# Three short matmuls between block 0 and the first paired block of an out-projection

## The chip, the cores and the metric

The kernel runs on one core of one Trainium2 chip. The metric is the device time of one execution in microseconds (us). Before the change three runs gave 822.88, 823.33 and 823.69 us, median 823.33. The profile is of one further execution of the same program.

## What is computed

The reference is one decoder block for a sequence of 512 tokens and a model width of 2048, in float32. Cut to what matters here:

```python
h = _rmsnorm(x, norm_g[l])
proj = h @ w_in[l]                       # queries, keys, values, gates, z
...                                      # two groups of attention heads -> y_a, y_b
x = x + jnp.concatenate([y_a, y_b], axis=-1) @ w_out[l]
...
return _rmsnorm(x, final_g)
```

The change lies in the product with `w_out`, a 512 x 2048 times 2048 x 2048 product, the last large stage.

## The kernel before, in words

All products of float32 data are made from pairs of words in fp32r, a high and a low one. `mm3` (line 121) issues three matmuls for one product: line 122 takes high by high, line 123 high by low, line 124 low by high. In the out-projection the stationary operand of a matmul is a 128 x 128 piece of the activations (`yh`, `yl`, `ph`, `pl`, `uh`, `ul`, `qh`, `ql`), and the moving operand is a piece of the weights (`whi`, `wlo`). Each matmul comes with its own load of the stationary operand; the trace shows it as LDWEIGHTS on a row of its own, PEld, and it runs beside the matmul before.

The weights come in by DMA as units of 128 x 1024 float32. ScalarE copies a unit to its high word, VectorE subtracts to get the low word (`load_unit`, line 85; `split_to`, line 957, for the out-projection; lines 958 and 959). The words go into tiles that are 1088 words wide per partition, and `words(place)` (line 82) chooses where in the tile the 1024 used words begin: `MOVING, EVEN, STILL = 0, 16, 32` (line 29). So the place sets at which word address a unit begins; `p_words` (line 964) does the same with tiles 2112 wide.

The 2048 output columns are four blocks of 512 (variable `n`).

- **Block 0** (the loop over `u` in range(8) behind `acc = banks(0)`) is a plain product: for each of 16 pieces of the contraction and each of four row tiles one `mm3`, its matmuls 512 columns wide. In between, `combos` (line 971) builds sums and differences of the activations: `p`, `u`, `q`.
- **Blocks 1, 2 and 3** (the loop `for n in range(1, 4)`) use a scheme with seven instead of eight half-size products on 2 x 2 sub-blocks ("12", "21", "22", "p", "u", "q", "w"). Each is one call of `product` (line 1123), or two calls for a half each in block 3: 8 pieces times 2 row tiles times 3 matmuls = 48 matmuls, each 256 columns wide. That makes 7 x 48 = 336 matmuls in a block and 1008 in the three. These are the paired blocks.

The first product of block 1 is "p", into the PSUM tile `ba` (named `oa` in the profile). Its stationary operands are `ph` and `pl`, the first unit of weights is `u3`, converted by `halves` (line 1072) while block 0 still runs.

Behind each product VectorE adds PSUM into sums in SBUF, and the next weights are converted. At the end of block 3 the rows are scaled by their norm (lines 1004 to 1036) and written out by DMA (line 1020).

Order: within an engine the instructions stand in an order that the framework's scheduler chose; `tc.issue_after(x)` puts what follows behind instruction `x` on its engine. In block 3 the order is nearly written out by hand in this way (`do`, `mm`). `recent["mm"]` is the last matmul that `mm3` issued.

Of the kernel before, what the change touches and what calls it, by code (L numbers as in the profile page):

```python
# [17 lines left out]
P = 128  # L18
# [17 lines left out]
def hybrid_block(ctx, tc, xT, xtm, w0, w1s, w2s, wz, wq, wkb, wo0, wos, cw1, cw2, cpos, rope, tabs, sinks, gT, fg, out):  # L36
    nc = tc.nc
    pe, act, dve, pool = nc.tensor, nc.scalar, nc.vector, nc.gpsimd
# [39 lines left out]
    def raw():  # L78
        raws[0] += 1
        return weights(f"raw{raws[0] % 3}")  # L80
# [38 lines left out]
    recent = {}  # L119
# [56 lines left out]
    for k in range(KT):  # L176
# [7 lines left out]
        for i in range(4):  # L184
            o = i * P
# [140 lines left out]
    for u in range(KT // 2):  # L326
# [15 lines left out]
        for j in range(2):  # L342
            k = 2 * u + j
            for i in range(4):
                o = j * 512 + i * P
# [562 lines left out]
    for i in range(8):  # L908
# [8 lines left out]
        if i == 7:  # L917
# [3 lines left out]
            yh = [so1.tile([P, S], F32R, name=f"yh{f}") for f in range(16)]  # L921
# [121 lines left out]
    def banks(n):  # L1043
        if n % 2 == 0:
            return [psf1.tile([P, S], F32, name="oa", tag="oa") for t in range(2)] + \
                   [psp.tile([P, S], F32, name="pj", tag="pj") for t in range(2)]
        return [psf2.tile([P, S], F32, name="oa", tag="oa") for t in range(4)]
# [24 lines left out]
    def halves(raw, to=None):  # L1072
        hi, lo = to or words(MOVING)
        split_to(hi, lo, raw)
        return hi, lo

    def as_pair(b):
        return b.rearrange("p (t c) -> p t c", c=256)

    fgt = []  # L1080
    for n in range(1, 4):
        xs.append([late(2 * n - 2 + T) for T in range(2)])
        src = wos[n - 1]
        ba, bb, bx, bc = [as_pair(b) for b in banks(n)]
# [3 lines left out]
        def scratch():  # L1088
            return so.tile([P, 2, 256], F32, name="e", tag="e", bufs=3)

        def load(dst, quarter, g):
            last["dma"] = nc.sync.dma_start(dst, src[quarter, g]).ins
            return dst
# [29 lines left out]
        def product(bank, units, op, new, ts=(0, 1)):  # L1123
            for m in range(8):
                hi, lo = units[m // 4]
                cs = slice((m % 4) * 256, (m % 4) * 256 + 256)
                ah, al = ops[op, m]
                for t in ts:
                    r = slice(t * P, (t + 1) * P)
                    mm3(bank[:, t, :], ah[:, r], al[:, r], hi[:, cs], lo[:, cs], new and m == 0 and t == ts[0],  # L1130
                        m == 7 and t == ts[-1], not new)
# [3 lines left out]

        u3 = [halves(load(raw(), 0, g)) for g in range(2)]
        e3 = scratch()
        if n < 3:
            product(ba, u3, "p", True)
            act.activation(e3, ba, AF.Copy)  # L1140
# [232 lines left out]
```

## Time and profile before

| | |
|---|---|
| three runs, us | 822.88, 823.33, 823.69 |
| the profiled execution, us | 822.97 |
| its span, first to last instruction, us | 821.2 |
| mean granted TensorE clock | 0.997 |
| TensorE (PE) busy, us | 808.1 |
| VectorE (DVE) busy, us | 665.9 |
| ScalarE (ACT) busy, us | 484.4 |
| block 0 of the out-projection, us from the span's start | 652.5 to 694.7 |
| paired blocks, us from the span's start | 694.7 to 813.4 |
| last sums, norms and writes, us | 813.4 to 821.2 |

How to read it: the span lies inside the device time, which has 822.97 - 821.2 = 1.8 us more around it. A row of the timeline has the start, the length, the engine, the line in the kernel, the operation and the tiles, out<-in. Matmuls are pipelined: the length of a row is that of one matmul from its start to the end of its drain, and the next one starts long before that. What a stream of matmuls costs is therefore the distance from one start to the next, called the pitch here. An engine that is busy 98% by this count can still run at two different pitches.

Where two addresses are compared, they are in words of 4 bytes within a partition, and only the remainder by 64 is given. The distance of a matmul is the start address of its moving operand less the start address of the stationary operand that is loaded while it runs, that is, of the next matmul's. The addresses of the tiles are those of the built program; the profile doesn't show them.

### The profile page before, as it was taken

What the parts mean: (1) busy time and instruction counts of PE and PEld (TensorE: products, weight loads), DVE (VectorE), ACT (ScalarE), POOL (GpSimd) and SP (SyncE); (2) the same over time, 40 slices, a digit from 0 to 9 for tenths busy, and PEclk for the clock granted to TensorE, in tenths of its full rate; (3) what the DMA queues carried; (4) which work ended last, traced back from release to release, by engine and by line L of the source; (5) the groups of instructions that cost most, each with busy time, mean ns of one, the idle gap of its engine ahead of it and who ended that gap; (6) DMA issues with size and microseconds to landing.
All of it is one profiled execution on the core that took longest, in us unless ns stands there. A gap on an engine that the chain in (4) does not pass through costs nothing.

```text
span 821.2 us, 14128 instructions
## 1 busy us (share of the span) xinstructions
PE 808.1 (98%) x5278; PEld 736.2 (90%) x5278; DVE 665.9 (81%) x1326; ACT 484.4 (59%) x1026; POOL 66.6 (8%) x54
## 2 busy tenths in 40 slices
PE   9999999999999999999999999999999999999996
PEld 8788898989999999999988888888888888999996
DVE  7869786867889899899877598887777899768895
ACT  6734456564767787777665465544553747453545
POOL 4500002010000000000011211011001000000000
PEclk9999999999999999999999999999999999999998
DMA  9655886898321332432732322222223167596835
GB/s 330 203 197 167 288 301 192 285 346 296 99 91 29 114 105 89 144 109 77 262 114 83 116 78 77 69 87 54 75 81 100 52 180 278 128 264 154 275 57 205
DMA packets 52116, 128.30 MB, mean 156 GB/s; under 512 B 4944, under 2 KB 17232, under 8 KB 52048
## 3 DMA queue, kind: packets, MB, share of 16 engines
q1 hardware_dynamic: 50032, 120.59, 43.9%
q0 software_dynamic: 1728, 6.29, 4.5%
q8 instruction: 41, 0.67, 0.3%
q10 hardware_dynamic: 288, 0.52, 0.2%
q14 instruction: 27, 0.22, 0.1%
HBM read 110.31 MB, written 17.07 MB: 155 GB/s over the span
## 4 chain that ended last, share of the span: by engine, by line
PE 92%; ACT 2%; DVE 2%; DMA 1%; issue 1%; POOL 1%; SPq 0%; DVEq 0%
PE pj L124 17%; PE pj L123 17%; PE pj L122 16%; PE oa L122 5%; PE oa L123 5%; PE oa L124 5%; PE bank L124 4%; PE bank L122 4%; PE bank L123 4%; PE sp L557 3%; PE tp L595 2%; PE tp L879 2%; DMA xr<-xT 1%; PE spb L844 1%; PE spb L845 1%; PE bank L236 1%
## 5 line engine op out<-in xcount | busy, mean ns | idle before, releaser
L124 PE MATMUL pj<-xh,wlo 128*128 128x512 f32 (+1 forms) x560 | 194.9, 348 | 1.8 <-DVE wlo L635 1.8
L122 PE MATMUL pj<-xh,whi 128*128 128x512 f32 (+1 forms) x560 | 194.6, 348 | 0.0
L123 PE MATMUL pj<-xl,whi 128*128 128x512 f32 (+1 forms) x560 | 194.5, 347 | 0.0
L96 DVE TENSOR_TENSOR wlo<-raw,whi 128x1024 fp32r<-128x1024 f32 (+2 forms) x102 | 115.6, 1137 | 34.2 <-ACT whi L95 33.5
L95 ACT ACTIVATE whi<-raw 128x1024 fp32r<-128x1024 f32 (+1 forms) x101 | 95.0, 944 | 77.1 <-PE pj L123 23.4
L124 PEld LDWEIGHTS pj<-xh,wlo 128*128 128x128 f32 x560 | 105.4, 188 | 15.0 <-DVE wlo L635 2.4
L123 PEld LDWEIGHTS pj<-xl,whi 128*128 128x128 f32 x560 | 105.3, 188 | 13.2 <-issue 0.9
L122 PEld LDWEIGHTS pj<-xh,whi 128*128 128x128 f32 x560 | 105.3, 188 | 12.2
L635 DVE TENSOR_TENSOR wlo<-raw,whi 128x1024 fp32r<-128x1024 f32 x49 | 59.5, 1220 | 9.5 <-ACT whi L634 9.4
L634 ACT ACTIVATE whi<-raw 128x1024 fp32r<-128x1024 f32 x49 | 51.2, 1055 | 21.7 <-PE pj L123 10.7
L122 PE MATMUL oa<-whi,yh 128*128 128x256 f32 (+1 forms) x168 | 50.5, 302 | 0.6 <-ACT yh L954 0.6
L123 PE MATMUL oa<-wlo,yh 128*128 128x256 f32 (+1 forms) x168 | 50.8, 302 | 0.0
L124 PE MATMUL oa<-whi,yl 128*128 128x256 f32 (+1 forms) x168 | 50.2, 302 | 0.0
L858 ACT ACTIVATE ttb<-ttb,sums 128x256 f32<-128x256 f32 (+1 forms) x64 | 30.1, 471 | 27.0 <-DVE sums L851 26.5
L525 ACT ACTIVATE ph<-tp 128x512 fp32r<-128x512 f32 x56 | 32.3, 592 | 14.5 <-PE tp L595 8.4
L123 PE MATMUL bank<-wlo,xh 128*128 128x256 f32 (+1 forms) x128 | 40.1, 315 | 0.0
L124 PE MATMUL bank<-whi,xl 128*128 128x256 f32 (+1 forms) x128 | 39.8, 313 | 0.0
L526 DVE TENSOR_TENSOR pl<-tp,ph 128x512 fp32r<-128x512 f32 x56 | 37.9, 685 | 1.8 <-ACT ph L525 1.6
L122 PE MATMUL bank<-whi,xh 128*128 128x256 f32 (+1 forms) x128 | 36.5, 317 | 1.3 <-ACT whi L95 1.3
L122 PE MATMUL bank<-xh,whi 128*128 128x512 f32 x96 | 36.7, 392 | 0.4 <-ACT whi L95 0.3
L123 PE MATMUL bank<-xl,whi 128*128 128x512 f32 x96 | 36.9, 390 | 0.0
L573 ACT ACTIVATE tt<-tt,sums 128x128 f32<-128x128 f32 (+3 forms) x64 | 35.3, 554 | 1.5 <-DVE sums L563 1.4
(357 smaller groups left out, 2173.9 us busy)
## 6 DMA issues: line engine op xcount, KB each, us to landing
raw<-wz SPq DMA_DIRECT2D x36, 512.0 KB, 3.8
raw<-wq SPq DMA_DIRECT2D x28, 512.0 KB, 3.7
raw<-cw SPq DMA_DIRECT2D x16, 512.0 KB, 4.8
raw<-wos SPq DMA_DIRECT2D x12, 512.0 KB, 4.4
rw<-wos SPq DMA_DIRECT2D x10, 512.0 KB, 5.4
xr<-xT SPq DMA_DIRECT2D x16, 256.0 KB, 4.8
raw<-w SPq DMA_DIRECT2D x8, 512.0 KB, 4.1
fd<-ft SPq DMA_DIRECT2D x4, 1024.0 KB, 6.1
```

Source lines behind the costliest of these rows:

```text
L95: last["hi"] = act.activation(hi[:, :width], rw[:, :width], AF.Copy).ins
L96: last["lo"] = dve.tensor_tensor(out=lo[:, :width], in0=rw[:, :width], in1=hi[:, :width].bitcast(F32), op=ALU.subtract).ins
L122: pe.matmul(ps, ah, bh, start=first, stop=False, skip_group_check=go_on)
L123: pe.matmul(ps, ah, bl, start=False, stop=False, skip_group_check=go_on)
L124: recent["mm"] = pe.matmul(ps, al, bh, start=False, stop=last, skip_group_check=go_on).ins
L525: act.activation(ph, tp, AF.Copy)
L526: dve.tensor_tensor(out=pl, in0=tp, in1=ph.bitcast(F32), op=ALU.subtract)
L557: pe.matmul(sp[:, a:b], qq[:, qs], kk[0][:, ko:ko + b - a], start=pi == 0, stop=pi == 2)
L573: act.activation(tv, tv, AF.Exp, bias=mn[:, i, 1 + w:2 + w], scale=-1.0, accum_out=dn[:, i, 1 + w:2 + w])
L634: act.activation(hi, src, AF.Copy)
L635: last["lo"] = dve.tensor_tensor(out=lo, in0=src, in1=hi.bitcast(F32), op=ALU.subtract).ins
L858: act.activation(tv, tv, AF.Exp, bias=mn[:, e, v:v + 1], scale=-1.0, accum_out=dn[:, e, v:v + 1])
```

## The change

A helper `step_in` issues three matmuls behind the last one of block 0 and ahead of the "p" product of block 1. All three have the same stationary operand, the first 128 columns of `yh[1]`, and as moving operand 256 columns of the same tile that begin 48, 64 and 32 words further on. They write the first half of the PSUM tile `ba`, each with start and stop set; the first matmul of the "p" product starts that tile anew, so nothing of theirs is kept. The engines' other instructions and their order are the same in both programs.

```diff
@@ -1077,6 +1077,11 @@
     def as_pair(b):
         return b.rearrange("p (t c) -> p t c", c=256)
 
+    def step_in(bank):
+        with tc.issue_after(recent["mm"]):
+            for o in (48, 64, 32):
+                pe.matmul(bank[:, 0, :], yh[1][:, 0:P], yh[1][:, o:o + 256], start=True, stop=True)
+
     fgt = []
     for n in range(1, 4):
         xs.append([late(2 * n - 2 + T) for T in range(2)])
@@ -1135,6 +1140,8 @@
 
         u3 = [halves(load(raw(), 0, g)) for g in range(2)]
         e3 = scratch()
+        if n == 1:
+            step_in(ba)
         if n < 3:
             product(ba, u3, "p", True)
             act.activation(e3, ba, AF.Copy)
```

In the changed program the three stand on line 1083, between the last line 124 of block 0 and the first line 122 of block 1. The lines behind them move down by five, and those behind the call by seven.

## The prediction

> **What bounds the kernel now.** I read the page first, then the busy time by stage, then the timeline of TensorE.
>
> ```profile
> PE 808.1 (98%) x5278; PEld 736.2 (90%) x5278; DVE 665.9 (81%) x1326; ACT 484.4 (59%) x1026; POOL 66.6 (8%) x54
> PE 92%; ACT 2%; DVE 2%; DMA 1%; issue 1%; POOL 1%; SPq 0%; DVEq 0%
> ```
>
> The first row is busy time by engine, the second the chain that ended last: TensorE holds 92% of it. The paired blocks and what follows them (columns: stretch, its length, then busy time of PE, PEld, DVE, ACT and POOL with counts, granted clock, DMA share and rate):
>
> ```profile
> 694.73:813.40 118.67, 118.67 (x1009) 118.66 (x1007) 94.46 (x117) 60.13 (x88) 8.73 (x10) 1.00 0.66 186
> ```
>
> ```profile
> 813.40:821.20 7.80, 0.22 (x2) 0.01 (x1) 1.80 (x5) 2.14 (x5) 0.00 (x0) 0.71 0.40 149
> ```
>
> In the paired blocks (first row) PE is busy in every microsecond at full clock (1.00), and behind it comes a tail of 7.8 us that starts when PE ends. So the time can only fall there if the matmuls follow each other faster. Whether they can is told by the pitch, the distance between starts. The first two rows are the first and the last of the 1008 paired matmuls; the other two are the first and the last of 116 matmuls of an earlier stage, of the same shape and at the same distance (48):
>
> ```profile
> 694.73 0.28 PE L122 MATMUL oa<-whi,ph 128*128 128x256 f32 x1
> ...
> 813.34 0.28 PE L124 MATMUL oa<-whi,ql 128*128 128x256 f32 x1
> ```
>
> ```profile
> 104.61 0.28 PE L122 MATMUL bank<-whi,xh 128*128 128x256 f32 x1
> ...
> 117.64 0.28 PE L236 MATMUL bank<-whi,F 128*128 128x256 f32 x1
> ```
>
> The paired blocks run at (813.34 - 694.73) / 1007 = 117.8 ns. The earlier stage runs at (117.64 - 104.61) / 115 = 113.3 ns. Neither stream has a pause. So the same kind of matmul has **two steady paces**, 4.5 ns apart, at one clock and one distance of addresses; by their rows neither width, type nor distance decides which. What decides must be history, and there the trace can be read like an experiment, since the head loop often mixes in a matmul at another distance.
>
> **What the three matmuls do.** Their distances follow from the diff alone: the stationary operand begins at the tile's start, the moving one 48, 64 and 32 words behind, so 48, 0 and 32 by the remainder. After them "p" begins at 48 again, as all 1008 do. The question is what the series 48, 0, 32, 48 does to a stream at the slow pace. The head loop has it, where one attention matmul (L601) stands between projection matmuls: by the addresses of the tiles in the built program the load for L601 makes the distance of the matmul ahead of it 0, and the load behind L601 makes its own 32; all others there have 48.
>
> ```profile
> 352.53 0.28 PE L123 MATMUL pj<-xl,whi 128*128 128x256 f32 x1
> ...
> 354.65 0.28 PE L123 MATMUL pj<-xl,whi 128*128 128x256 f32 x1
> 354.77 0.28 PE L601 MATMUL op<-ph,VH 128*128 128x256 f32 x1
> 354.89 0.28 PE L124 MATMUL pj<-xh,wlo 128*128 128x256 f32 x1
> ...
> 355.59 0.28 PE L124 MATMUL pj<-xh,wlo 128*128 128x256 f32 x1
> ...
> 356.95 0.28 PE L124 MATMUL pj<-xh,wlo 128*128 128x256 f32 x1
> ```
>
> Ahead of it 18 pitches take 354.65 - 352.53 = 2.12 us: 117.8 ns, slow. The two odd distances stand at 354.65 and 354.77. Then six pitches take 0.70 us, and from 355.59 on 12 pitches take 1.36 us: 113.3 ns, **fast**. No wait lies between. But a slow stream isn't the same at every matmul: every third weight load on PEld is longer. Where the loads stand that run beside the second paired matmul and beside the matmul with distance 0 in two passages (busy us, then mean ns of one):
>
> ```profile
> L124 PEld LDWEIGHTS oa<-whi,pl 128*128 128x128 f32 x1 | 0.2, 192 | 0.0
> ```
>
> ```profile
> L601 PEld LDWEIGHTS op<-ph,VH 128*128 128x128 f32 x1 | 0.2, 188 | 0.0
> ```
>
> ```profile
> L601 PEld LDWEIGHTS op<-ph,VH 128*128 128x128 f32 x1 | 0.2, 192 | 0.0
> ```
>
> Here (first row) the 0 will stand in place of the second paired matmul, and that one has a long load, 192 ns. In the passage above (second row) the 0 has a short one, 188: another of the three places. A second passage (third row) has 192, so the same place as here:
>
> ```profile
> 213.52 0.28 PE L122 MATMUL pj<-xh,whi 128*128 128x256 f32 x1
> 213.64 0.28 PE L123 MATMUL pj<-xl,whi 128*128 128x256 f32 x1
> 213.76 0.29 PE L601 MATMUL op<-ph,VH 128*128 128x256 f32 x1
> 213.89 0.28 PE L124 MATMUL pj<-xh,wlo 128*128 128x256 f32 x1
> 214.00 0.28 PE L122 MATMUL pj<-xh,whi 128*128 128x256 f32 x1
> 214.12 0.28 PE L123 MATMUL pj<-xl,whi 128*128 128x256 f32 x1
> 214.24 0.28 PE L124 MATMUL pj<-xh,wlo 128*128 128x256 f32 x1
> ```
>
> Here 48, 0 and 32 start at 213.52, 213.64 and 213.76. The pitches behind them (0.11, 0.12, 0.12) are those of the passage above, where it was on its way to the fast pace; another odd distance cuts it off before it gets there. So I take it that the stream goes fast, and this last step is inferred.
>
> **The sum.**
> - Added: three matmuls on a PE that has no idle time to hide them. From the passage, 213.89 - 213.52 = 0.37 us.
> - On the way to the fast pace six pitches take 0.70 us instead of 6 x 113.3 ns = 0.68: 0.02 us.
> - Gained: 1008 x 4.49 ns (117.79 less 113.30) = 4.52 us, if the fast pace holds to the end. All paired matmuls have distance 48, so no address throws them out.
> - Tail: unchanged at 7.8 us, it starts from PE's end. Around the span nothing changes.
>
> 0.37 + 0.02 - 4.52 = -4.13 us. The profiled execution took 822.97, so 818.84; the median of the runs is 0.36 above it, so **819.2**.
>
> **What hides under PE, and if that cover goes.** The weights must be converted 4% faster. That the converters wait for PE and not the reverse is in the waits of the paired blocks (engine and line, for whom; us in total, times, longest):
>
> ```profile
> ACT whi L958 <- PE oa L124: 21.6, 17, 1.8
> ```
>
> So most units follow PE's pace. The tightest place is in block 3, where VectorE has other sums ahead of a low word:
>
> ```profile
> 791.09 1.06 ACT L1198 ACTIVATE whi<-rw 128x1024 fp32r<-128x1024 f32 x1 [1.67 <-PE pj L124]
> ```
>
> ```profile
> 796.38 1.22 DVE L1201 TENSOR_TENSOR wlo<-rw,whi 128x1024 fp32r<-128x1024 f32 x1
> ```
>
> ```profile
> 797.91 0.28 PE L122 MATMUL oa<-whi,yh 128*128 128x256 f32 x1
> 798.02 0.28 PE L123 MATMUL oa<-wlo,yh 128*128 128x256 f32 x1
> ```
>
> The low word is done at 796.38 + 1.22 = 797.60; its matmul starts at 798.02, and the load for that matmul when the one before starts, at 797.91. VectorE's series of sums there hangs on the high word that ScalarE begins at 791.09, when PE lets go of a buffer, some 60 pitches earlier; so it loses 60 x 4.5 ns = 0.27 us of its lead of 0.31. That just holds by this estimate; what a miss costs is the second rival. DMA and output writes keep the same lead to within this figure, since buffers come free faster in step with PE.
>
> **A rule that speaks against it.** The Trainium skill, "TensorE: Matmul & The Clock Gate", under "Step-by-step: what each phase is for", says that weight load and moving operand have read ports of their own and that loading the next weights takes nothing from the running matmul. By that rule distances would not matter, and the sum would be the 0.37 us alone. The trace disagrees so far: 113.3 against 117.8 ns for one shape at one clock.
>
> **The rivals.**
> - *The step does nothing.* The stream is slow after the three too: the entry from 512 columns counts differently from the passage's, or distances don't decide at all. For it: the second passage is cut off, so the last step was never seen from that place, and in the head loop the stationary address jumps where here it is the moving one. Against it: the same pitches so far. Price: 0.37 us that nothing hides, so slower than before, 823.7. It decides if the pitch is still 117.8 ns ten matmuls in. (The skill's rule above is the strict form of it.)
> - *Fast, then thrown back.* A pause of PE draws the pace anew. In the earlier stage the fast stretch ended so:
>
> ```profile
> 117.75 0.28 PE L237 MATMUL bank<-wlo,F 128*128 128x256 f32 x1
> 118.05 0.38 PE L236 MATMUL bank<-whi,F 128*128 128x256 f32 x1
> 118.46 0.38 PE L123 MATMUL bank<-wlo,xh 128*128 128x256 f32 x1
> 118.68 0.28 PE L124 MATMUL bank<-whi,xl 128*128 128x256 f32 x1
> ...
> 121.04 0.28 PE L124 MATMUL bank<-whi,xl 128*128 128x256 f32 x1
> ```
>
>   Starts 0.30 and 0.41 us apart, and from 118.68 on 20 pitches take 2.36 us: slow. If the place at 798 pauses PE, its last 131 matmuls are slow again: 131 x 4.5 ns = 0.6 us given back, so 819.8; an earlier pause gives back more, up to all.
> - *A third, slower pace.* The pitches at 0 and 32 are longer: 213.64 to 214.24 is 0.60 us for five, 120 ns. If the stream stayed there, 1008 x 2.2 ns = 2.2 us more, with the 0.37: 825.9. Against it: no stretch of this width stays there in the trace. It decides if the pitch rises and doesn't come back.
>
> **Chances.** Fast to the end 0.72, thrown back 0.10 (0.09 of it still over 0.2% faster), nothing 0.13 (0.04 of it for distances that don't matter at all), third pace 0.05. A measurement of this kernel tells about 0.2% (1.6 us) from no change. So faster 0.81, same 0.14 (nothing, and a throw-back at the start), slower 0.05. The runs before lie within 0.8 us of each other, so the low end is 818.5; the high end takes in most throw-backs, 822.0; outside are the first and the third rival and the worst throw-backs, 0.2 together.
>
> **What would show it.** Right: line 1083 three times with pitches near 0.12, 0.12 and 0.13, some six pitches behind them near 0.117, then 113.3 ns; the last matmul about 114.5 us after the first of line 1083 (before, 118.6 us from the first paired one to the last); PE without idle time in block 3, where the low words are on line 1208 then; the tail 7.8 us. Wrong: 117.8 ns behind line 1083, a pause of PE in block 2 or 3 with a change of pitch behind it, or a tail that grows by what PE gains.

## The result, and the profile after

| us | before | after |
|---|---|---|
| median | 823.61 | 820.32 |
| lowest and highest | 822.88, 824.75 | 819.75, 821.86 |
| runs | 8 | 8 |
| the profiled execution | 822.97 | 820.54 |
| its span | 821.2 | 818.8 |

After to before is 0.9958, with an interval of 0.9949 to 0.9968: 3.29 us faster by the medians. That is over the 0.2% named in the prediction.

Where it came from stands in the timeline of TensorE of the changed kernel: the three matmuls of line 1083 in one row, three of the first paired ones, and the very last.

```profile
696.02 0.52 PE L1083 MATMUL oa<-yh 128*128 128x256 f32 x3
696.37 0.28 PE L122 MATMUL oa<-whi,ph 128*128 128x256 f32 x1
...
696.73 0.28 PE L122 MATMUL oa<-whi,ph 128*128 128x256 f32 x1
...
697.07 0.28 PE L122 MATMUL oa<-whi,ph 128*128 128x256 f32 x1
...
810.93 0.28 PE L124 MATMUL oa<-whi,ql 128*128 128x256 f32 x1
```

Read the starts, not the lengths: each row is 0.28 us long before and after. The three take 696.37 - 696.02 = 0.35 us. The first three pitches behind them take 0.36 us together, the next three (to 697.07) 0.34, which is 113.3 ns each. From the first of line 1083 to the last matmul pass 810.93 - 696.02 = **114.91 us**; before, 118.61 from the first paired matmul to the last. Behind the last matmul the span goes on for 818.8 - 810.93 = 7.9 us, as before (821.2 - 813.34 = 7.9).

The loads show the pace in one row each. Loads of the stationary operand on PEld, grouped by line, in the stretch from 700 to 750 us; the last number before the idle time is the mean length in ns. Of before:

```profile
L124 PEld LDWEIGHTS oa<-whi,yl 128*128 128x128 f32 x93 | 17.9, 192 | 0.0
L123 PEld LDWEIGHTS oa<-wlo,yh 128*128 128x128 f32 x93 | 17.5, 188 | 0.0
```

Of after:

```profile
L124 PEld LDWEIGHTS oa<-whi,yl 128*128 128x128 f32 x94 | 17.6, 188 | 0.0
```

At the slow pace the loads of one line in three (L124) are 192 ns long, those of the others 188; at the fast pace the long ones are gone.

One thing came that the prediction had bet against, a pause of TensorE in block 3. Its timeline again:

```profile
795.55 0.28 PE L124 MATMUL oa<-whi,yl 128*128 128x256 f32 x1
795.67 0.28 PE L122 MATMUL oa<-whi,yh 128*128 128x256 f32 x1
796.08 0.38 PE L123 MATMUL oa<-wlo,yh 128*128 128x256 f32 x1
796.30 0.28 PE L124 MATMUL oa<-whi,yl 128*128 128x256 f32 x1
```

The starts at 796.08 and 796.30 are 0.41 and 0.22 behind the ones ahead of them, instead of 0.113: 0.40 us lost. The matmul at 796.08 reads the low word `wlo`, and behind it the pace is fast again. The chain of work that ended last, in order of time (start, us, what), shows where that word comes from:

```profile
748.32 1.07 ACT whi L958
...
768.15 9.07 DMA rw<-wos
777.30 1.07 ACT whi L1205
...
783.88 5.52 DMA rw<-wos
789.51 1.07 ACT whi L1205
...
794.89 1.14 DVE wlo L1208
796.08 0.38 PE oa L123
```

So the chain is no longer TensorE's alone. It leaves TensorE at 748 us, runs over the converters and over two transfers into `rw`, and comes back to TensorE with that low word. On the page TensorE's share of the chain falls from 92% to 85%:

```profile
PE 85%; DVE 5%; DMA 4%; ACT 3%; issue 2%; POOL 1%; SPq 0%; DVEq 0%; ACTq 0%; POOLq 0%
```

ScalarE's row says the same, the time in brackets being the idle time ahead of it and what ended it:

```profile
789.51 1.06 ACT L1205 ACTIVATE whi<-rw 128x1024 fp32r<-128x1024 f32 x1 [1.56 <-DMA rw<-wos]
```

Before, the same instruction waited for a buffer that PE let go ("[1.67 <-PE pj L124]", in the prediction).

The two profiles add up: in after, the paired stretch with its three extra matmuls is 118.61 - 114.91 = 3.70 us shorter, the tail is the same, and the stages ahead of the change ended 696.02 - 694.73 = 1.29 us later: 2.4 us, the difference of the two spans. That 1.29 us lies ahead of the first instruction that the change touches. Part of it is the same effect elsewhere: the stage that ran at 113.3 ns before (104.61 to 117.64 in the prediction) ran at the slow pace here. The first and the fifteenth start of a stretch of it:

```profile
105.32 0.28 PE L124 MATMUL bank<-whi,xl 128*128 128x256 f32 x1
...
106.97 0.28 PE L124 MATMUL bank<-whi,xl 128*128 128x256 f32 x1
```

14 pitches in 1.65 us are 117.9 ns. In the profiles of this study the first of the added matmuls starts anywhere from 694.36 to 697.34 us, though the edits of all kernels lie behind that point or at it. A single run therefore can't be read by its time; the experiments below are read by the stretch from the first matmul on line 1083 to the last one.

### The profile page after: what moved, and what is told of

Read it like the earlier page. It is cut to its first block, busy times and chain, and to the rows that moved or that the text cites. A ratio compares the mean times of both kernels' runs of the same rounds, so it can differ in the third digit from the quotient of the medians.

```text
span 818.8 us, 14134 instructions
## 1 busy us (share of the span) xinstructions
PE 805.6 (98%) x5281; PEld 733.7 (90%) x5281; DVE 666.6 (81%) x1326; ACT 483.6 (59%) x1026; POOL 67.7 (8%) x54
## 4 chain that ended last, share of the span: by engine, by line
PE 85%; DVE 5%; DMA 4%; ACT 3%; issue 2%; POOL 1%; SPq 0%; DVEq 0%; ACTq 0%; POOLq 0%
PE pj L124 16%; PE pj L123 16%; PE pj L122 16%; PE bank L124 4%; PE bank L122 4%; PE oa L123 4%; PE bank L123 4%; PE oa L122 4%; PE oa L124 3%; PE sp L557 3%; DMA rw<-wos 2%; PE tp L595 2%; PE tp L879 2%; DMA xr<-xT 1%; PE spb L844 1%
## 5 line engine op out<-in xcount | busy, mean ns | idle before, releaser
L124 PE MATMUL pj<-xh,wlo 128*128 128x512 f32 (+1 forms) x560 | 194.9, 348 | 1.8 <-DVE wlo L635 1.8
L124 PEld LDWEIGHTS pj<-xh,wlo 128*128 128x128 f32 x560 | 105.4, 188 | 15.0 <-DVE wlo L635 2.4
L124 PE MATMUL oa<-whi,yl 128*128 128x256 f32 (+1 forms) x168 | 49.5, 298 | 0.0
L124 PE MATMUL bank<-whi,xl 128*128 128x256 f32 (+1 forms) x128 | 39.9, 314 | 0.0
```

The lines of the kernel that those rows point to most:

```text
L124: recent["mm"] = pe.matmul(ps, al, bh, start=False, stop=last, skip_group_check=go_on).ins
```

## Experiments

Theory: the paired stream keeps the pace in which it starts, a pause aside, and the distances of the first few matmuls choose it. Rivals: any short matmuls between the 512-wide stream and the paired one do it; or where the addresses lie matters in another way than by the remainder; or the pace is chance. The last one weighs, since the earlier stage near 105 us, which no edit touches, started behind a pause and ran at 113.4 to 113.5 ns over its 125 pitches in six of the fourteen profiles of this study and at 117.8 in eight. The paired stream starts without a pause, and its pace repeats: eight profiles have 48, 0, 32 ahead of it (the two of the change, 112-128-96, and the five kernels further down that keep the three steps), and all eight start fast; the kernel before and 48-48-48, with no odd distance, are slow. No time of the change on record is over 821.94 us, and none of the kernel before is under 822.72. The other four series below were profiled once each, so for each of them alone chance isn't excluded. The pause of block 3 has theories of its own, further down.

| steps (remainders) | 1st step to last matmul, us | pace | time of the run or median, us |
|---|---|---|---|
| 48, 0, 32 (the change) | 114.91; again 115.29 | fast | 820.32; again 820.2 |
| 48, 48, 48 | 118.96 | slow | 823.35 |
| 32, 0, 48 | 118.96 | slow | 822.95 |
| 0, 32 | 118.84 | slow | 823.85 |
| 48, 0 | 115.25 | fast | 820.54 |
| 48, 48, 0 | 118.96 | slow | 824.17 |
| 112, 128, 96 (48, 0, 32) | 115.43 | fast to 796 | 821.37 |

### All three at 48

```diff
-            for o in (48, 64, 32):
+            for o in (48, 48, 48):
```

> The three matmuls stay, but all at distance 48 (offsets 48, 48, 48), the distance of the paired blocks. Theory 1, the series of distances moves the stream from one pace to the other: no odd distance, so no move; pitch 117.8 ns from the first to the last of the paired matmuls, no pause in block 3, the paired stretch 118.6 us plus 0.35. Rival, three more short matmuls or the 0.36 us that they last are enough, whatever their distances: pitch 113.3 ns as in the changed kernel, paired stretch some 115 us.

One run, 823.35 us. The timeline of TensorE, the steps, the first paired matmul and the last one:

```profile
694.77 0.52 PE L1083 MATMUL oa<-yh 128*128 128x256 f32 x3
695.12 0.28 PE L122 MATMUL oa<-whi,ph 128*128 128x256 f32 x1
...
813.73 0.28 PE L124 MATMUL oa<-whi,ql 128*128 128x256 f32 x1
```

118.96 us, of which the three matmuls take 0.35 and the 1008 the same 118.61 as before. So three short matmuls alone cost 0.35 us and gain nothing; **their addresses** make the 4.05 us between 118.96 and 114.91 (the pause of the change, 0.40, already taken off). Two programs with the same instructions in the same order, and only the moving start of three matmuls different: that excludes widths, counts and queues as the cause. The Trainium skill's rule that was weighed in the prediction ("TensorE: Matmul & The Clock Gate", "Step-by-step: what each phase is for") says that the next weights' load takes no read bandwidth from the running matmul. Read as saying that distances don't matter, it would have made these two kernels equal, and the measurement decides against that reading here. Whether a load takes read bandwidth from a matmul is not shown.

### The same distances in reverse

```diff
-            for o in (48, 64, 32):
+            for o in (32, 64, 48):
```

> The same three distances in the reverse order: 32, 0, 48. If order decides (theory 1, a state that each distance moves on by a step), this need not end in the fast pace; I expect 117.8 ns, with 0.6 to 0.7 odds. If it is enough that some odd distances stand between block 0 and block 1 (rival), the pitch is 113.3 ns as in the changed kernel.

One run, 822.95 us. Timeline:

```profile
694.36 0.52 PE L1083 MATMUL oa<-yh 128*128 128x256 f32 x3
...
813.32 0.28 PE L124 MATMUL oa<-whi,ql 128*128 128x256 f32 x1
```

118.96 us, slow. The same three distances in another order did nothing in this profile, so the order counts, unless by chance, and passing a 0 isn't enough.

### Without the first, and without the last

```diff
-            for o in (48, 64, 32):
+            for o in (64, 32):
```

> The first of the three is left out: 0, 32. Theory 1: the 0 now falls at another of the three places of the slow stream, the first paired matmul. In the passage at 354.65 us of the kernel before the 0 fell at yet another place than in the changed kernel and the stream went fast too, so I expect 113.3 ns here and 0.12 us less in all than with three. If the place decides: 117.8 ns.

One run, 823.85 us. Two steps now, so the row has x2:

```profile
695.39 0.40 PE L1083 MATMUL oa<-yh 128*128 128x256 f32 x2
...
814.23 0.28 PE L124 MATMUL oa<-whi,ql 128*128 128x256 f32 x1
```

118.84 us, slow. This was a miss: 0 and 32 right behind the 512-wide stream don't do it.

```diff
-            for o in (48, 64, 32):
+            for o in (48, 64):
```

> The last of the three is left out: 48, 0. Two passages of the kernel before bear on it: a lone 0 in a slow stream (305.83 us) was followed by pitches near 114 ns, a lone 0 in a fast stream by 118. Theory 1 by these: 113.3 ns, and the 32 isn't needed. If only the full series 0, 32 moves the stream: 117.8 ns.

One run, 820.54 us:

```profile
695.68 0.40 PE L1083 MATMUL oa<-yh 128*128 128x256 f32 x2
...
810.93 0.28 PE L124 MATMUL oa<-whi,ql 128*128 128x256 f32 x1
```

115.25 us with a pause in block 3 as after the change: fast. So the 32 isn't needed here, where the first paired matmul (48) stands in its place; and beside 0, 32, which stayed slow, it looks as if the 48 ahead of the 0 is needed.

### The 0 one place later

```diff
-            for o in (48, 64, 32):
+            for o in (48, 48, 64):
```

> The steps are 48, 48, 0, so that the 0 is the third behind block 0 and no longer the second; no 32 follows, as in the kernel without the 32, which went to the pitch of 113.3 ns. Theory, as far as the runs so far bear it: what counts is a 48 ahead of the 0 while the stream is in its 117.8 ns pace, and the place of the 0 doesn't; then some six pitches behind the step are near 117 and the rest 113.3 ns, the last matmul is about 115 us behind the first of line 1083, and a pause near 796 is to be seen. Rival: only one place in the period of three works (the place beside the long load); then 117.8 ns to the end, the last matmul about 119 us behind the first step, no pause. Chances 0.6 and 0.4.

One run, 824.17 us:

```profile
695.59 0.52 PE L1083 MATMUL oa<-yh 128*128 128x256 f32 x3
...
814.55 0.28 PE L124 MATMUL oa<-whi,ql 128*128 128x256 f32 x1
```

118.96 us: slow, and the likelier expectation missed. A 48 ahead isn't enough; with no 32 in either kernel, the 0 worked as the second matmul behind block 0 and not as the third. This agrees with the rival of one place in three. The loads bear on it: in the kernel without the 32 the load beside the 0 is that of the first paired matmul, and in its group between 695.6 and 696 us it has the long length:

```profile
L122 PEld LDWEIGHTS oa<-whi,ph 128*128 128x128 f32 x1 | 0.2, 193 | 0.0
```

In the kernel of this section the first paired matmul's load also runs beside the 0, and is short:

```profile
L122 PEld LDWEIGHTS oa<-whi,ph 128*128 128x128 f32 x1 | 0.2, 188 | 0.0
```

But it is no proof. The passage at 354.65 in the prediction has the 0 beside a short load too, and went fast; there a 32 follows, which is missing here. A kernel with 48, 48, 0, 32 would tell the place from the 32; it wasn't run.

### Distances 64 words further on

```diff
-            for o in (48, 64, 32):
+            for o in (112, 128, 96):
```

> Offsets 112, 128 and 96 in place of 48, 64 and 32: each moving operand begins 64 words further on, so that the remainders by 64 are the same. If only the remainder by 64 words counts: the same pitches as in the changed kernel (117, 122, 117, 117, 122, then 113.3 ns). If the whole distance counts, or another unit such as 128 words, the series differs and the stream may stay at 117.8 ns.

One run, 821.37 us. The steps, then the pause of block 3 and what follows it:

```profile
696.30 0.52 PE L1083 MATMUL oa<-yh 128*128 128x256 f32 x3
...
795.95 0.28 PE L122 MATMUL oa<-whi,yh 128*128 128x256 f32 x1
796.32 0.38 PE L123 MATMUL oa<-wlo,yh 128*128 128x256 f32 x1
796.54 0.28 PE L124 MATMUL oa<-whi,yl 128*128 128x256 f32 x1
...
797.72 0.28 PE L122 MATMUL pj<-whi,yh 128*128 128x256 f32 x1
...
799.84 0.28 PE L122 MATMUL pj<-whi,yh 128*128 128x256 f32 x1
...
811.73 0.28 PE L124 MATMUL oa<-whi,ql 128*128 128x256 f32 x1
```

The stream goes fast, so 64 words further on make no difference to how it starts. Whether a shorter step than 64 words would do the same (32, say) wasn't tried. And here the rival that was priced in the prediction stands in the trace: behind the pause, 18 pitches from 797.72 to 799.84 take 2.12 us, 117.8 ns. The stream went into the pause fast and came out of it slow. 115.43 us to the last matmul.

### A lone 0 ahead of block 2

```diff
-    def step_in(bank):
+    def step_in(bank, steps=(48, 64, 32)):
         with tc.issue_after(recent["mm"]):
-            for o in (48, 64, 32):
+            for o in steps:
...
+        if n == 2:
+            step_in(ba, (64,))
```

> As the changed kernel, and ahead of the first product of block 2 one more matmul at distance 0. In the kernel before a lone 0 in a fast stream was followed by pitches of 118 ns (225.31 us and four more places). Theory 1: fast in block 1, slow at 117.8 ns from block 2 on; 672 x 4.5 ns = 3.0 us of the gain are gone, time about that of the kernel before less 1.1 us. Rival, the fast pace is a stable state that only a pause can end: a single pitch is longer and the stream stays at 113.3 ns.

One run, 821.05 us. The three steps ahead of block 1, the added matmul with what follows, and the last one:

```profile
696.37 0.52 PE L1083 MATMUL oa<-yh 128*128 128x256 f32 x3
...
734.83 0.28 PE L1083 MATMUL oa<-yh 128*128 128x256 f32 x1
...
735.06 0.29 PE L123 MATMUL oa<-wlo,ph 128*128 128x256 f32 x1
735.19 0.28 PE L124 MATMUL oa<-whi,pl 128*128 128x256 f32 x1
...
811.40 0.28 PE L124 MATMUL oa<-whi,ql 128*128 128x256 f32 x1
```

115.03 us with one matmul more and a pause in block 3: the fast stream takes a single 0, stretches a few pitches (735.06 to 735.19) and goes on fast. I had expected it to fall to the slow pace from there. So what the head loop's odd distances do to a stream isn't a rule that can be carried over matmul by matmul.

### The change again, and the cover in block 3

The changed kernel was timed again beside a variant that takes one of VectorE's sums from ahead of the low word that was late, and puts it behind:

```diff
-            do(more, 0, ch, r12)
             for t in range(2):
                 mm(bxt[t], u5, "u", True, (t,))
             u1.append(pair())
             do(both, u1[1], r22[1])
+            do(more, 0, ch, r12)
```

> The changed kernel once more, timed on the same chip as the kernel with the moved sum. Pitch 113.3 ns behind the three, a pause of PE of 0.3 to 0.8 us in block 3 ahead of the first low word of w, and 0.35 to 0.45% under the kernel before.

> As the changed kernel, but in block 3 one VectorE addition into the combined weights (more, 0) stands behind the low word that PE waited for, not ahead of it. Theory, the pause at 795.7 us is VectorE's series of work behind the late landing of rw: the low word is done 1.1 us earlier, the pause goes (0.4 us), the last matmul starts 114.5 us after the first of line 1083, and the time is 0.4 us under the changed kernel's. Rival, the pause is the DMA's alone, since the high word waits for it: the pause stays.

The changed kernel: 820.2 us median of 5 (819.32 to 821.94), before 824.05 of 9, ratio 0.9953 (0.9939 to 0.9966). Its pause, in the timeline:

```profile
795.93 0.28 PE L122 MATMUL oa<-whi,yh 128*128 128x256 f32 x1
796.72 0.39 PE L123 MATMUL oa<-wlo,yh 128*128 128x256 f32 x1 [0.51 <-DVE wlo L1208]
```

0.79 us between two starts this time, 0.41 in the first profile: the result repeats, and the size of the pause varies from one execution to the next.

The variant: 821.16 us (820.49 to 823.12), ratio 0.9967 (0.9954 to 0.9979). No gain; 115.61 us from the first step to the last matmul (695.28 to 810.89), with pauses at five places instead of one, and the fast pace behind each. At the old place the starts are now 0.16 and 0.22 apart (from 795.51), which loses 0.15 us instead of 0.40; but a new pause at 789.7, ahead of a low word for the product "u", loses 0.35. The high word that the moved sum should have cleared the way for still starts late, since it waits for a transfer:

```profile
789.52 1.06 ACT L1205 ACTIVATE whi<-rw 128x1024 fp32r<-128x1024 f32 x1 [1.21 <-DMA rw<-wos]
793.29 1.06 ACT L1205 ACTIVATE whi<-rw 128x1024 fp32r<-128x1024 f32 x1 [2.71 <-DMA rw<-wos]
```

And the sum put back is itself late for the next words, which shows as a pause at 803.82 of 0.37 us. My theory that VectorE's order alone held the word falls: the moved sum shrank one pause and others came.

### What block 3 waits for: VectorE's work, or the transfers

Two more edits, alone and together. The first puts the two loads of input rows of block 3 behind its last weight loads (in blocks 1 and 2 they stay where they were, so the expectation's "each paired block" says too much):

```diff
         r22 = [load(rw(), 3, g) for g in range(2)]
-        load_rows()
         if n < 3:
+            load_rows()
             product(bb, [halves(r) for r in r22], "22", True)
...
         else:
             r12 = [load(raw(), 1, g) for g in range(2)]
+            load_rows()
```

The second takes four products with the gain (L1011) off the start of block 3: two go into the scaling of rows 2 and 3, two come later in the block. The lines shown leave out where the scaling of rows 2 is put:

```diff
-        if n == 3:
-            dve.scalar_tensor_tensor(out=v, in0=v, scalar=r, in1=fgt[1][:, 512:1024], op0=ALU.mult, op1=ALU.mult)
+        if n == 3 or t > 1:
+            k = (n - 2) * 512
+            dve.scalar_tensor_tensor(out=v, in0=v, scalar=r, in1=fgt[1][:, k:k + 512], op0=ALU.mult, op1=ALU.mult)
...
             u0 = [halves(r22[0])]
-            for t in (2, 3, 0, 1):
-                do(times_g, 2, t)
...
             for t in range(2):
+                do(times_g, 2, t)
+            for t in range(2):
                 mm(bat[t], u4, "12", False, (t,))
```

> Takes the two loads of input rows that each paired block issues ahead of its last weights, and that are wanted only late in the block, and puts them behind these weights. Question: is the pause of 0.4 to 0.8 us near 796 in block 3 due to the DMA transfers of the sums of weights that land at 777.2 and 789.4? Theory: two things bind VectorE's series of sums from 778.3 on, the landing at 777.2 and VectorE's own 2.5 us of products with the gain that end at 778.3; so DMA alone gives about nothing: the pause stays at 0.35 to 0.8, the last matmul 114.9 to 115.3 us behind the first of line 1083. Rival: DMA alone binds; then the landing is 1 us or more earlier, ScalarE's high word at 789.5 begins earlier, no pause, and 114.5 us.

> Takes the four products with the gain (2.5 us of VectorE) off the start of block 3: two are folded into the scaling of rows 2 and 3, two stand later in the block. Theory as for the run before: VectorE is only one of two things that bind the series, so alone it gives little, pause 0.3 to 0.8 us, 114.9 to 115.3 us from the first of line 1083 to the last matmul. Rival: VectorE's work alone binds: series about 1.3 us earlier, no pause, 114.5 us, and the tail behind the last matmul still 7.8 us.

> Both edits together. Theory: the series of sums starts about 1.3 us earlier, the low word near 796 is done at least 0.3 us ahead of its matmul, no pause; the last matmul 114.5 us behind the first of line 1083, tail 7.8 us; 0.4 to 0.8 us under the changed kernel by the trace, about 819.7 to 820 with the spread of the stages ahead. Rival: the sum of the DMA traffic of block 3 binds, wherever its parts stand: the pause stays, or another place pauses instead, and the time is the changed kernel's, 820.3 within 0.5.

| | first weights of block 3 (ScalarE starts), us behind the first step | 1st step to last matmul, us | us |
|---|---|---|---|
| the change | 777.30 - 696.02 = 81.28 | 114.91 | 820.32 median of 8 |
| rows later | 780.12 - 697.34 = 82.78 | 116.20 | 823.16, one run |
| gain later | 776.91 - 695.27 = 81.64 | 114.84 | 819.72, one run |
| both | 778.67 - 697.15 = 81.52 | 115.36 | 821.59 median of 9 (819.48 to 823.74) |

Both together: ratio 0.9968 (0.9954 to 0.9981), no better than the change. VectorE's first low word of block 3 in the kernel with the gain later:

```profile
778.01 1.23 DVE L1209 TENSOR_TENSOR wlo<-rw,whi 128x1024 fp32r<-128x1024 f32 x1 [2.21 <-ACT whi L1206]
```

and in the one with both:

```profile
779.77 1.23 DVE L1210 TENSOR_TENSOR wlo<-rw,whi 128x1024 fp32r<-128x1024 f32 x1 [3.15 <-ACT whi L1207]
```

VectorE was rid of 2.5 us of work and idled 2.21 us and 3.15 us instead, waiting for ScalarE's high word, which waited for the transfer into `rw`. With the rows moved, the high word started 1.5 us later (82.78 against 81.28), not earlier; that kernel paused first at 782.0 (0.46 us), went on slow, was fast again from 792.7 on, behind two pitches of 0.13 and 0.22 us, and stayed fast behind a second pause, of 0.74 us at 797.9. So the theory that both have to go was wrong, and "both" stands with its rival: in no order that was tried does the transfer land sooner. That the sum of the traffic sets when it lands, as the rival has it, is not shown; what would bring it sooner (fewer bytes, an earlier buffer) wasn't tried.

The kernel with both fell back as well. Its stream around the pause and at the end:

```profile
796.80 0.28 PE L122 MATMUL oa<-whi,yh 128*128 128x256 f32 x1
797.10 0.38 PE L123 MATMUL oa<-wlo,yh 128*128 128x256 f32 x1
...
798.50 0.28 PE L122 MATMUL pj<-whi,yh 128*128 128x256 f32 x1
...
812.51 0.28 PE L124 MATMUL oa<-whi,ql 128*128 128x256 f32 x1
```

798.50 to 812.51 is 14.01 us for the last 119 pitches: 117.7 ns. Of the seven profiles in which a fast stream has its first pause between 794.9 and 796.8 (the change twice, 48 and 0 alone, the lone 0, 112-128-96, gain later, both), five go on fast and two go on slow, and the length of the pause doesn't tell which: 0.35 us went on fast, 0.37 slow, 0.29 slow, 0.85 fast. The two kernels whose first pause comes earlier fit in: the one with the moved sum stayed fast, the one with the rows later went slow and then, at 792.7, fast again. So the pace behind a pause can't be told from these traces, neither here nor in the earlier stage.

## Why the prediction held, step by step

1. **TensorE bounds, and only its pitch can give.** Right up to 748 us, where the chain leaves TensorE. The pitch is the one thing that changed: 113.3 for 117.8 ns, in the same 0.28 us rows.
2. **The series 48, 0, 32, 48 takes a slow stream to the fast pace.** Right in outcome, with 48-48-48 as the control (118.96 against 114.91 us). The reason was only partly right, and luck had a share: by the same reasoning a gain was expected of 0, 32 and, as the likelier case, of 48-48-0, and neither came. That the 0 must be in the second place, as the second passage had it, is what the other orders point to, with one profile each; the 32 is not needed; and the idea that a 0 in itself moves a stream fell with the lone 0, the reverse order and 48-48-0. The rule that fits all runs, a 48 and then a 0 in the second place, comes from seven series and is a description, not a mechanism. Why addresses act on pace at all was never shown.
3. **The sum.** Three matmuls: 0.37 forecast, 0.35 measured. The way in, 0.02: right within a row's rounding. Gain, 4.52 forecast: the paired stretch of the change without its pause is 114.91 - 0.40 - 0.35 = 114.16 us, against 118.61 before, so 4.45. By profiles the stretch with the three matmuls gained 3.70 us where 4.13 was forecast; of the 0.43 between them the pause is 0.40.
4. **The cover.** This is the step that failed: "That just holds by this estimate", with a lead of 0.31 and a loss of 0.27. The low word was ready at 794.80 + 1.22 = 796.02 and due at 795.67 + 0.11 = 795.78:

```profile
794.80 1.22 DVE L1208 TENSOR_TENSOR wlo<-rw,whi 128x1024 fp32r<-128x1024 f32 x1
```

   That is 0.24 late; counted as in the prediction, from the load that starts with the matmul at 795.67, it is 0.35 late. The estimate let ScalarE's high word hang on a buffer that PE frees, and said that DMA keeps the same lead. Counted from the first paired matmul, the high word started at 791.09 - 694.73 = 96.36 us before and at 789.51 - 696.37 = 93.14 after: 3.22 us sooner. Its matmul came sooner by (797.91 - 694.73) - (795.67 - 696.37) = 3.88. VectorE's run that begins behind this high word and ends with the low word starts 4.20 us ahead of the latter in both (792.18 to 796.38, 790.60 to 794.80). The loss is 0.66 instead of 0.27 (0.31 less 0.66 is the 0.35), because the transfer, which before had landed at 790.92, 0.17 ahead of the high word's start, now came last, after PE's release. That the lead would have held with an earlier transfer is an estimate; no run shows it. The "tightest place" was the right one. The second rival foresaw the pause but not its cost: it counted up to 0.6 us for a slow pace behind it and nothing for the pause itself, and here the pause took 0.40 and the pace stayed fast.
5. **What a pause does.** Both profiles of the change kept the fast pace behind it, which is luck as far as the record shows; the rival's price of a throw-back showed in two other kernels (0.5 us over the last 119 pitches).
6. **The tail, and the stages around.** The tail is 7.9 us in both, as forecast. "Around the span nothing changes" holds, but the stages ahead vary by up to 3 us from one execution to the next, which is more than the 0.8 us that the first three runs of before showed; that widens the scatter of the times, with the change and without it.

By medians the change is worth 3.29 us and 3.85 the second time, about the 4.13 less the pause. The rivals "does nothing" (823.7) and "a third pace" (825.9) fall; the former is what the kernels with 48-48-48, with the reverse, with 0-32 and with 48-48-0 did, at 822.95 to 824.17 in one run each.

## What to carry to other kernels

When TensorE is busy in every microsecond, look at the distance between starts: a busy share of 98% hides two paces, and the loads' lengths (188 everywhere, or 192 at every third) tell which one runs. A stream's pace can be chosen by a few matmuls ahead of it, but only by trying: distances that differ in nothing but their order gave all or nothing. Before an engine is made 4% faster, follow the tightest lead back to the instruction that would be last if it went, transfers included, and don't assume that these keep step.

## What the runs showed of the hardware that was not expected

- Two steady pitches of one shape (128 x 128 stationary, 256 columns) at a granted clock of 1.00 in the stretch: 113.3 and 117.8 ns, 4.0%. At the slow one the record shows one load in three 4 ns longer, yet all three pitches are longer.
- Where the stream starts without a pause, the choice went with the start addresses of three matmuls ahead of it (48, 64, 32 fast in seven profiles of seven; 48, 48, 48 slow). 64 words more (112, 128, 96) changed nothing. By one profile each, it also goes with the order and with the place behind the wider stream.
- A pause of TensorE may draw the pace anew: two of seven fast streams went on slow. In the kernel with the rows later a slow stream turned fast behind two pitches of 0.13 and 0.22 us.
- The time ahead of the change varied by 3 us between profiles of programs nearly alike; one stage of it, behind a pause, ran at 113.4 to 113.5 ns in six of the fourteen profiles and at 117.8 in eight.
